# Layer 0's first weights loaded behind x's second tile, their high parts written by Pool and their low parts by VectorE, and the first zT half in two column parts

## The chip, the cores and the metric

The kernel runs as one program on one core of a Trainium2 chip. The metric is the device time of one launch in microseconds (us), the median of three runs; lower is better.

## What is computed

A trunk of two layers on 1024 tokens of width 1024, all in float32. Cut to what matters here:

```python
for l in range(DEPTH):                       # DEPTH = 2
    h = _rmsnorm(x, g_pre_mix[l])
    z = h @ w_in[l]                          # 1024 x 1280
    zf, zq, zk, zv, zm = jnp.split(z, splits, axis=-1)   # zf: the first 256 columns
    y_f = _fourier_mix(zf, w_fourier[l])     # FFT over tokens and channels, then w_fourier
    ...                                      # windowed attention on zq, zk, zv
    mkv = _rmsnorm(mem, g_mem[l]) @ w_mem_kv[l]          # keys and values of 256 memory rows
    ...                                      # memory attention with zm, then w_out and a residual
    ...                                      # SwiGLU with w_ffn_in, w_ffn_out and a residual
```

The change concerns the first of these products alone: `zf`, the first 256 columns of `h @ w_in[0]`, in layer 0.

## The kernel before

**Products in three passes.** TensorE multiplies in a rounded 32-bit format (`fp32r`). To keep precision, each operand is kept as a high part, its rounding, and a low part, what the rounding left. A product is three matmuls: high by high, high by low, low by high (`Acc.add`, L173). `split` (L160 to 163) makes the two parts: ScalarE (ACT) casts the high part (L162), and VectorE (DVE) or GpSimd (POOL) subtracts it for the low part (L163).

**The start of layer 0.** x comes in eight tiles of 128 tokens (`start_load`, L1339; five slots). For each, `start_tile` (L1343) squares and sums the tile on ACT (L311), turns the sum into a scale on POOL (L313, L314), and transposes the tile on TensorE in two groups of four 128x128 blocks, `hTp` (L325). Each group is split by ACT (L162) and DVE (L163) into the two parts of hT. Four tiles make a half of hT, 512 tokens wide.

The gain g_pre_mix is folded into the weights. `zf_load` (L521) calls `load_w` (L355): four transfers of 256 KB, each two k-blocks of 128 rows by 256 columns, into a ring of three raw slots (`raws`, L136). POOL scales each block in place (`scaled`, L353), ACT casts the high part of the pair, POOL subtracts for the low part, and only then is the slot free for a later load. The transfers stand behind x's fourth tile, and a fourth one behind the small tables and x's later tiles.

`zf(0)` (L524) then makes zT, 256 rows by 512 tokens: two row blocks of 24 matmuls each, 512 columns wide, then a split, then `pq` (a small product with the Fourier tables that `fourier_tables`, L503, has made through `abp`). The second half, `zf(1, 2)`, is made in two column parts of 256 tokens.

Between the two halves stands the memory's work (`Memory.make`, L472): two tiles of mem are loaded, squared (L300), normed on DVE (L305) and transposed (`mTp`, L450); eight transfers of w_mem_kv go through the same ring of three raw slots, each cast on ACT and subtracted on DVE; `kmp` and `vmp` are the products. Then `kvz_load` takes eight more blocks of w_in through the same ring (`load_w512`, L375: ACT and DVE for the even blocks, POOL and ACT for the odd ones).

**What sets the order.** The program is written as a sequence, and a scheduler then orders the instructions of each engine by a timeline of its own. Each engine runs its list in that order: an instruction that waits holds up what stands behind it. All loads named here are issued by SyncE (SP). From its ninth transfer on, SP waits before each issue for the transfer issued eight places before, and where a buffer is reused also for the engine that last read it. PSUM buffers come in pairs per tag (L42): `sc` holds zT, `pT` holds abp, mTp and pq, `pd` holds hTp, kmp and vmp.

Of the kernel before, what the change touches and what calls it, by code (L numbers as in the profile page):

```python
# [12 lines left out]
F32R = mybir.dt.float32r  # L13
# [3 lines left out]
ALU = mybir.AluOpType  # L17
AX = mybir.AxisListType

P = 128  # L20
# [38 lines left out]
def weave(*streams):  # L59

    order = []
    for si, units in enumerate(streams):
        order += [((i + 0.5) / len(units), si, i, u) for i, u in enumerate(units)]
    for *_, u in sorted(order, key=lambda o: o[:3]):
        u()
# [3 lines left out]
def tile_encoder(ctx: ExitStack, tc: tile.TileContext, T, C, out):  # L69
    nc = tc.nc  # L70
# [32 lines left out]
    def shaped(ap, shape):  # L103
        names = "abcde"[: len(shape)]
        dims = {c: d for c, d in zip(names, shape)}
        return ap.rearrange(f"p ({' '.join(names)}) -> p {' '.join(names)}", **dims) if len(shape) > 1 else ap

    def at(k, *shape, dt=F32):

        t = arenas[F32R if dt is F32R else F32]  # L110
        if dt is not F32R and k >= 8:
            k, t = (k - 8, flex["t"]) if k < 16 else (k - 8, t)
        o = int(k * 256)
        ap = t[:, o : o + math.prod(shape)]
        return shaped(ap.bitcast(dt) if dt is I32 else ap, shape)
# [16 lines left out]
    def run(k, n, step):  # L132
        return Ring(*[k + i * step for i in range(n)])


    raws, junks = run(0, 3, 2), Ring(56)  # L136
# [20 lines left out]
    f32 = lambda ap: ap.bitcast(F32)  # L157
    mm = nc.tensor.matmul

    def split(hi, lo, src, lo_eng=None):  # L160

        nc.scalar.copy(hi, src)  # L162
        return (lo_eng or nc.vector).tensor_tensor(out=lo, in0=src, in1=f32(hi), op=ALU.subtract)  # L163
# [16 lines left out]
    def cst(*shape):  # L180
# [20 lines left out]
        out=mask[:, 0:P], in_=mask[:, 0:P], pattern=[[1, P]], compare_op=ALU.is_ge,  # L201
# [4 lines left out]
        out=mask[:, 2 * P : 3 * P], in_=mask[:, 2 * P : 3 * P], pattern=[[-1, P]],  # L206
# [101 lines left out]
    def token_scale(x, t):  # L308

        ss = sm(1, "nss")  # L310
        nc.scalar.activation(junks(D // 2).bitcast(BF16), x, AF.Square, accum_out=ss)  # L311
        v = sm(1, "nrsv")
        nc.gpsimd.tensor_scalar(out=v, in0=ss, scalar1=1.0 / D, scalar2=EPS, op0=ALU.mult, op1=ALU.add)  # L313
        nc.gpsimd.tensor_tensor(out=rx[:, t : t + 1], in0=v, in1=mhalf[:, 0:1], op=ALU.pow)  # L314

    def norm_T(h, hT, t, tag="pd"):

        half, c = divmod(t, 4)
        if c == 0:
            hT[half] = [[at(32 * half + 16 * i + 8 * kg, 4, 512, dt=F32R) for kg in range(2)] for i in range(2)]  # L320
        for kg in range(2):
            pt = ps([4, P], "hTp", tag)
            for j in range(4):
                k = kg * 4 + j
                nc.tensor.transpose(pt[:, j, :], h[:, k * P : (k + 1) * P], ident)  # L325
            split(hT[half][0][kg][:, :, c * P : (c + 1) * P], hT[half][1][kg][:, :, c * P : (c + 1) * P], pt)
# [25 lines left out]
    def scaled(raw, g, k):  # L352
        nc.gpsimd.tensor_scalar(out=raw, in0=raw, scalar1=g[:, k : k + 1], scalar2=1.0, op0=ALU.mult, op1=ALU.mult)  # L353

    def load_w(w, c0, n, k, lo_eng=None, g=None):  # L355


        kn = 1024 // n
        kr = kn // 2
        res = []  # L360
        for k0 in range(0, NK, kn):
            hi, lo = at(k, kn, n, dt=F32R), at(k + 4, kn, n, dt=F32R)
            k += 8
            for j in range(0, kn, kr):
                raw = raws(kr, n)
                r0 = (k0 + j) * P
                nc.sync.dma_start(raw, w[r0 : r0 + kr * P, c0 : c0 + n].rearrange("(k p) c -> p k c", p=P))
                if g is not None:
                    for i in range(kr):
                        scaled(raw[:, i], g, k0 + j + i)  # L370
                split(hi[:, j : j + kr], lo[:, j : j + kr], raw, lo_eng)
            res += [(hi[:, i], lo[:, i]) for i in range(kn)]
        return res
# [122 lines left out]
    class Mix:  # L496
# [22 lines left out]
            self.PQ = {}  # L519

        def zf_load(self):  # L521
            self.wzf = load_w(self.win, 0, 256, 64, nc.gpsimd, self.g)

        def zf(self, half, parts=1):  # L524

# [813 lines left out]
    def start_load(t):  # L1339
        hx[t] = at(32 + 4 * (t % 5), D)  # L1340
        nc.sync.dma_start(hx[t], x_in[t])

    def start_tile(t):  # L1343

        token_scale(hx[t], t)
        norm_T(hx.pop(t), hT, t)
        if t + 5 < NT:
            start_load(t + 5)
# [3 lines left out]
    mix = Mix(0, hT, mem)  # L1352
    start_load(0)
    gains_T(gpT, T["g_pre_mix"], at(15, P))
    for t in range(1, 4):
        start_load(t)
    mix.zf_load()
    start_load(4)
    for t in range(4):
        start_tile(t)  # L1360
    mix.fourier_tables(58)
    prep()
    mem.make()
    weave([lambda t=t: start_tile(t) for t in range(4, 8)], [lambda: mix.zf(0)])

    for l in range(DEPTH):
        mix.zf(1, 2)
# [57 lines left out]
        if l + 1 < DEPTH:  # L1425
            mem = Memory(l + 1, 16, 0, 16, 28, "pT")
            mix = Mix(l + 1, nhT, mem)
# [83 lines left out]
```

## Time and profile before

| | |
|---|---|
| median of 3 runs | 2069.59 us (2065.72 to 2076.48) |
| the profiled execution | 2072.77 us |
| its span, first to last instruction | 2070.9 us |
| mean granted TensorE clock | 0.981 |
| TensorE (PE) busy | 2001.5 us, 97% |
| VectorE (DVE) busy | 1546.8 us, 75% |
| ScalarE (ACT) busy | 1061.7 us, 51% |
| GpSimd (POOL) busy | 714.1 us, 34% |

The 1.9 us between the profiled execution's own time and its span lie around the instructions. PE is matmul; PEld is the loading of a weight block into TensorE, which overlaps PE. In a row of the timeline stand the start, the length (of all the instructions that the row merges), the engine, the line, the operation, output and input, the shape, and the count; in square brackets stands the idle time before it and what ended it. PEclk is the clock that TensorE was granted, as a share of full speed. SPq rows are issues of transfers, not the transfers.

### The profile page before, as it was taken

How to read it: one execution, taken by the hardware profiler on the slowest of the kernel's cores; microseconds unless marked ns; L12 is line 12 of the kernel's file. 1: busy time of each engine (PE TensorE's matmuls, PEld its weight loads, DVE VectorE, ACT ScalarE, POOL GpSimd, SP SyncE). 2: the span in 40 equal slices, each digit the busy share in tenths (PEclk: the TensorE clock that was granted, in tenths of full speed). 3: DMA queues.
4: the chain of work that ended last, by engine and by line, in shares of the span. 5: the costliest groups of instructions: out<-in, count | busy, mean ns of one | idle time of the engine just before them, and what ended most of it. 6: DMA issues, size and time to landing. Idle time of an engine off the chain costs nothing.

```text
span 2070.9 us, 28456 instructions
## 1 busy us (share of the span) xinstructions
PE 2001.5 (97%) x9587; PEld 1638.0 (79%) x9587; DVE 1546.8 (75%) x2496; ACT 1061.7 (51%) x2250; POOL 714.1 (34%) x819
## 2 busy tenths in 40 slices
PE   7999999899999999999999989997999999999998
PEld 6877777678888888887888768775888888878886
DVE  5556767888787786768876776579887787778767
ACT  6466777643333333455545677775433333345542
POOL 4354445433343333002423544363342342320002
PEclk9999999899999999999999999998999999999999
DMA  6110222423233233879841122233332233269974
GB/s 212 48 57 31 103 97 102 143 77 107 89 120 97 97 112 104 297 266 332 281 175 39 57 67 93 83 123 121 97 126 95 87 132 97 97 217 342 305 257 155
DMA packets 173634, 286.47 MB, mean 138 GB/s; under 512 B 15496, under 2 KB 73392, under 8 KB 173488
## 3 DMA queue, kind: packets, MB, share of 16 engines
q1 hardware_dynamic: 165424, 265.78, 38.7%
q10 hardware_dynamic: 8064, 18.88, 2.4%
q8 instruction: 75, 1.23, 0.2%
q14 instruction: 71, 0.58, 0.1%
HBM read 218.02 MB, written 66.58 MB: 137 GB/s over the span
## 4 chain that ended last, share of the span: by engine, by line
PE 85%; DVE 4%; DMA 3%; ACT 3%; POOL 3%; issue 2%; SPq 0%; DVEq 0%; POOLq 0%; ACTq 0%
PE fo L1277 19%; PE qz L1142 12%; PE qx L1142 11%; PE qy L1142 11%; PE mo L173 7%; PE qw L1142 6%; PE kvp L173 4%; PE qp L173 4%; PE zT L173 2%; PE pT L808 2%; PE sc L771 1%; DVE arena_r L163 1%; PE av L823 1%; PE av L816 1%; PE mav L916 1%
## 5 line engine op out<-in xcount | busy, mean ns | idle before, releaser
L162 ACT CAST arena_r<-arena_f 128x512 fp32r<-128x512 f32 (+2 forms) x714 | 411.5, 598 | 631.1 <-PE qz L1142 119.8
L163 DVE TENSOR_TENSOR arena_r<-arena_f,arena_r 128x512 fp32r<-128x512 f32 x632 | 476.5, 775 | 138.0 <-ACT arena_r L162 129.7
L1277 PE MATMUL fo<-arena_r 128*128 128x512 f32 x1848 | 424.7, 391 | 5.8 <-ACT arena_r L162 5.8
L1277 PEld LDWEIGHTS fo<-arena_r 128*128 128x128 f32 x1848 | 347.0, 188 | 78.8 <-ACT arena_r L162 4.4
L1142 PE MATMUL qy<-arena_r 128*128 128x512 f32 x1056 | 263.7, 400 | 16.5 <-ACT arena_r L162 11.1
L1142 PEld LDWEIGHTS qy<-arena_r 128*128 128x128 f32 x1056 | 203.3, 193 | 62.6 <-ACT arena_r L162 11.8
L1132 DVE TENSOR_TENSOR arena_f<-arena_f 128x512 f32<-128x512 f32 x220 | 201.9, 924 | 11.5 <-DMA arena_f<-in_w_ffn_in 5.0
L1142 PE MATMUL qz<-arena_r 128*128 128x512 f32 x704 | 199.1, 395 | 2.5 <-ACT arena_r L162 1.9
L1162 POOL TENSOR_TENSOR arena_f<-arena_f 128x512 f32<-128x512 f32 x44 | 71.8, 1633 | 313.7 <-ACT arena_f L1147 313.7
L1142 PEld LDWEIGHTS qz<-arena_r 128*128 128x128 f32 x704 | 134.2, 191 | 31.9 <-ACT arena_r L162 2.6
L1142 PE MATMUL qx<-arena_r 128*128 128x512 f32 x528 | 127.9, 390 | 0.4 <-ACT arena_r L162 0.4
L1142 PE MATMUL qw<-arena_r 128*128 128x512 f32 x528 | 127.3, 389 | 0.0
L1142 PE MATMUL qx<-big,arena_r 128*128 128x512 f32 x528 | 126.8, 389 | 0.0
L1142 PEld LDWEIGHTS qx<-arena_r 128*128 128x128 f32 x528 | 99.2, 188 | 21.7 <-ACT arena_r L162 1.2
L1142 PEld LDWEIGHTS qx<-big,arena_r 128*128 128x128 f32 x528 | 99.1, 188 | 20.6
L1142 PEld LDWEIGHTS qw<-arena_r 128*128 128x128 f32 x528 | 99.1, 188 | 20.6
L1142 PE MATMUL qz<-big,arena_r 128*128 128x512 f32 x352 | 115.2, 389 | 0.0
L221 POOL TENSOR_SCALAR rrsv<-rss 128x1 f32<-128x1 f32 x32 | 17.7, 554 | 259.3 <-ACT arena_f L334 207.3
L173 PE MATMUL qp<-big,arena_r 128*128 128x512 f32 x384 | 99.5, 404 | 2.0 <-POOL big L163 2.0
L173 PE MATMUL mo<-big,arena_r 128*128 128x512 f32 x384 | 101.4, 400 | 0.0
L1194 POOL TENSOR_TENSOR arena_f<-arena_f,flex 128x512 f32<-128x512 f32 x32 | 52.5, 1640 | 139.7 <-DVE arena_f L1174 101.0
L173 PE MATMUL mo<-arena_r 128*128 128x512 f32 x384 | 100.2, 401 | 0.3 <-POOL arena_r L163 0.3
(245 smaller groups left out, 3532.8 us busy)
## 6 DMA issues: line engine op xcount, KB each, us to landing
arena_f<-in_w_ffn_out SPq DMA_DIRECT2D x264, 256.0 KB, 4.6
arena_f<-in_w_ffn_in SPq DMA_DIRECT2D x88, 512.0 KB, 3.6
actd<-arena_f SPq DMA_DIRECT2D x154, 256.0 KB, 3.7
arena_f<-actd SPq DMA_DIRECT2D x154, 256.0 KB, 4.6
arena_f<-in_w_in SPq DMA_DIRECT2D x40, 256.0 KB, 2.8
arena_f<-in_x SPq DMA_DIRECT2D x16, 512.0 KB, 4.8
arena_f<-in_w_out SPq DMA_DIRECT2D x32, 256.0 KB, 2.7
pmd<-arena_f ACTq DMA_DIRECT2D x32, 256.0 KB, 2.0
```

The source lines that it names most:

```text
L162: nc.scalar.copy(hi, src)
L163: return (lo_eng or nc.vector).tensor_tensor(out=lo, in0=src, in1=f32(hi), op=ALU.subtract)
L173: mm(self.dst, a, b, start=self.i == 0, stop=self.i == self.n - 1)
L771: mm(pt, lhs, self.kst[g][i][:, k0 * P : k1 * P], start=i == 0, stop=i == 1)
L808: nc.tensor.transpose(pT[:, h, :], es_[h // 2][:, h % 2, j * P : j * P + P], ident)
L816: mm(av[64 * s : 64 * s + 64, 0 : 2 * P], self.v32[:, k0 + j], rhs, start=j == 0, stop=j == nk - 1)
L823: mm(av, lhs, p_, start=j == 0 and i == 0, stop=j == nk - 1 and i == 1)
L1132: nc.vector.tensor_tensor(out=s, in0=a, in1=b, op=op)
L1142: mm(pt, a, b, start=start and n == 0, stop=n == 11, skip_group_check=not start)
L1162: nc.gpsimd.tensor_tensor(out=self.v, in0=self.v, in1=self.s2, op=ALU.add)
L1194: (G if i in (0, 3) else V).tensor_tensor(out=a[i], in0=c, in1=g[i], op=ALU.mult)
L1277: mm(pt, ab[:, 0, x, sl], ab[:, 1, y], start=new and first and j == 0, stop=last and j == 2, skip_group_check=not new)
```

## The change

The weights of layer 0's `zf` no longer go through `load_w`. For each block of 128x256, POOL's scaling writes its product straight into the high part's `fp32r` buffer, and DVE makes the low part in one instruction, raw times gain minus high part. ACT has no part in it, and the scaling in place and POOL's subtraction are gone. Layer 1 keeps `load_w`. The loads are called behind x's second tile rather than behind its fourth, and `zf(0)` becomes `zf(0, 2)`: two parts of 256 tokens, so 96 matmuls of 256 columns in the place of 48 of 512.

```diff
         def zf_load(self):
-            self.wzf = load_w(self.win, 0, 256, 64, nc.gpsimd, self.g)
+            if self.l:
+                self.wzf = load_w(self.win, 0, 256, 64, nc.gpsimd, self.g)
+                return
+            self.wzf = []
+            for k0 in (0, 4):
+                hi, lo = at(64 + 2 * k0, 4, 256, dt=F32R), at(68 + 2 * k0, 4, 256, dt=F32R)
+                for j in (0, 2):
+                    raw = raws(2, 256)
+                    r0 = (k0 + j) * P
+                    nc.sync.dma_start(raw, self.win[r0 : r0 + 2 * P, 0:256].rearrange("(k p) c -> p k c", p=P))
+                    for i in range(2):
+                        g = self.g[:, k0 + j + i : k0 + j + i + 1]
+                        h = hi[:, j + i]
+                        nc.gpsimd.tensor_scalar(out=h, in0=raw[:, i], scalar1=g, scalar2=1.0, op0=ALU.mult, op1=ALU.mult)
+                        nc.vector.scalar_tensor_tensor(
+                            out=lo[:, j + i], in0=raw[:, i], scalar=g, in1=f32(h), op0=ALU.mult, op1=ALU.subtract
+                        )
+                self.wzf += [(hi[:, i], lo[:, i]) for i in range(4)]
...
     start_load(0)
     gains_T(gpT, T["g_pre_mix"], at(15, P))
-    for t in range(1, 4):
+    start_load(1)
+    mix.zf_load()
+    for t in range(2, 5):
         start_load(t)
-    mix.zf_load()
-    start_load(4)
     for t in range(4):
         start_tile(t)
...
-    weave([lambda t=t: start_tile(t) for t in range(4, 8)], [lambda: mix.zf(0)])
+    weave([lambda t=t: start_tile(t) for t in range(4, 8)], [lambda: mix.zf(0, 2)])
```

The scheduler answers with another order on every engine, over about the first fifth of the program and in a small stretch of layer 1. Lines of the changed kernel behind L538 are 17 higher than before.

On TensorE, at the start of the program, before (hTp_5 and 6 are x's first tile, 9 and 10 its second, 13 and 14 its third, 17 and 18 its fourth; zT_48 and zT_49 are the two row blocks of zT; abp the Fourier tables):

```order
L325 MATMUL hTp_10_168<-const_81,arena_f_73 128x128 x4
L325 MATMUL hTp_13_181<-const_81,arena_f_73 128x128 x4
L514 MATMUL abp_19_218<-arena_f_73 128x64
L514 MATMUL abp_20_224<-arena_f_73 128x64
L325 MATMUL hTp_14_188<-const_81,arena_f_73 128x128 x4
L325 MATMUL hTp_17_201<-const_81,arena_f_73 128x128 x4
L514 MATMUL abp_21_231<-arena_f_73 128x64
L514 MATMUL abp_22_237<-arena_f_73 128x64
L173 MATMUL zT_48_494<-arena_r_72 128x512
L173 MATMUL zT_49_521<-arena_r_72 128x512
L325 MATMUL hTp_18_208<-const_81,arena_f_73 128x128 x4
```

And of the changed kernel, from the same row on:

```order
L325 MATMUL hTp_10_168<-const_81,arena_f_73 128x128 x4
L173 MATMUL zT_48_494<-arena_r_72 128x256
L173 MATMUL zT_49_521<-arena_r_72 128x256
L325 MATMUL hTp_13_181<-const_81,arena_f_73 128x128 x4
L173 MATMUL zT_48_494<-arena_r_72 128x256 x11
L173 MATMUL zT_49_521<-arena_r_72 128x256 x8
L173 MATMUL zT_48_494<-arena_r_72 128x256
L173 MATMUL zT_49_521<-arena_r_72 128x256 x2
L325 MATMUL hTp_14_188<-const_81,arena_f_73 128x128 x4
L173 MATMUL zT_48_494<-arena_r_72 128x256 x5
L514 MATMUL abp_19_218<-arena_f_73 128x64
L514 MATMUL abp_20_224<-arena_f_73 128x64
```

zT's first matmuls moved from behind the fourth tile's first transposes and all four abp to right behind the second tile's; 28 of the 96 narrow ones stand before the first abp.

On ACT, further on, before (mTp are the transposes of the memory; the casts of arena_f 128x512 are those of w_mem_kv, whose eight transfers are here called kv0 to kv7, but for the second of the first row's three, which is the fourth pair of w_in's blocks; so that row is kv0, w_in, kv1):

```order
L162 CAST arena_r_72<-arena_f_73 128x512 x3
L162 CAST arena_r_72<-mTp_29_316 128x4x128
L162 CAST arena_r_72<-mTp_30_323 128x4x128
L162 CAST arena_r_72<-arena_f_73 128x512
L162 CAST arena_r_72<-mTp_34_337 128x4x128
L162 CAST arena_r_72<-arena_f_73 128x512 x2
L162 CAST arena_r_72<-zT_48_494 128x512
L162 CAST arena_r_72<-zT_49_521 128x512
L162 CAST arena_r_72<-mTp_35_344 128x4x128
```

And of the changed kernel, where kv0 and kv1 have been cast further up (the first row is kv2 to kv4; zT_52 and zT_53 are the second column part):

```order
L162 CAST arena_r_72<-arena_f_73 128x512 x3
L162 CAST arena_r_72<-zT_52_564 128x256
L162 CAST arena_r_72<-arena_f_73 128x512
L162 CAST arena_r_72<-zT_53_591 128x256
L162 CAST arena_r_72<-arena_f_73 128x512
L162 CAST arena_r_72<-mTp_29_316 128x4x128
L162 CAST arena_r_72<-mTp_30_323 128x4x128
L162 CAST arena_r_72<-arena_f_73 128x512
L162 CAST arena_r_72<-mTp_34_337 128x4x128
L390 ACTIVATE big_72_812<-arena_f_73,const_81 128x512
L162 CAST arena_r_72<-mTp_35_344 128x4x128
```

Before, the casts of the first two mTp stand behind those of kv0 and kv1; now they stand behind those of kv0 to kv6, and zT's casts stand ahead of them.

## Prediction

> **What bounds the kernel now.** I read the page first, then the waits of TensorE, then windows of 20 us.
>
> ```profile
> span 2070.9 us, 28456 instructions
> PE 2001.5 (97%) x9587; PEld 1638.0 (79%) x9587; DVE 1546.8 (75%) x2496; ACT 1061.7 (51%) x2250; POOL 714.1 (34%) x819
> ```
>
> PE is busy all but 69.4 us of the span, so a change in the order of loads can win no more than a part of that, and what half clock costs. Where these lie near the change, the windows tell (PE busy, PEld, DVE, ACT, POOL, granted clock, share of the DMA engines, GB/s):
>
> ```profile
> 0.00:20.00 20.00, 10.30 (x45) 8.51 (x45) 7.22 (x20) 14.41 (x31) 12.62 (x29) 0.84 0.88 287
> 20.00:40.00 20.00, 18.84 (x98) 15.90 (x99) 15.69 (x29) 13.76 (x27) 7.85 (x13) 0.91 0.54 172
> 40.00:60.00 20.00, 16.68 (x122) 16.44 (x121) 10.77 (x18) 12.86 (x24) 9.10 (x12) 0.86 0.48 145
> 140.00:160.00 20.00, 17.08 (x85) 14.53 (x86) 16.57 (x32) 11.96 (x35) 7.93 (x12) 0.91 0.01 2
> ```
>
> In the first 20 us PE stands idle for 9.7, in the next 1.2, in the third 3.3. DMA is close to full in the first window (0.88) and about half used in the next two. 0.5% of the time is 10.3 us, about what a measurement of this kernel can tell from no change: the whole idle time of the first 20 us is less than that.
>
> **The start.** These rows of the timeline carry the first two terms.
>
> ```profile
> 7.23 1.06 ACT L311 ACTIVATE arena_f<-arena_f 128x1024 bf16<-128x1024 f32 x1 [0.74 <-DMA arena_f<-in_x]
> 9.84 0.33 SPq L240 DMA_DIRECT2D const<-in_sink  x1
> 10.60 0.33 SPq L438 DMA_DIRECT2D arena_f<-in_mem  x1
> 10.88 1.85 POOL L353 TENSOR_SCALAR arena_f<-arena_f,const 128x256 f32<-128x256 f32 x4
> 11.93 0.69 DVE L163 TENSOR_TENSOR arena_r<-hTp,arena_r 128x512 fp32r<-128x512 f32 x1 [0.83 <-ACT arena_r L162]
> 15.74 2.50 POOL L163 TENSOR_TENSOR arena_r<-arena_f,arena_r 128x512 fp32r<-128x512 f32 x2
> 17.71 1.22 PE L173 MATMUL zT<-arena_r 128*128 128x512 f32 x2 [1.17 <-ACT arena_r L162]
> 19.92 7.03 PE L173 MATMUL zT<-arena_r 128*128 128x512 f32 x22
> 20.41 1.28 DVE L305 SCALAR_TENSOR_TENSOR arena_f<-arena_f,nrs 128x1024 f32<-128x1024 f32 x1 [1.12 <-issue]
> 25.84 0.94 POOL L353 TENSOR_SCALAR arena_f<-arena_f,const 128x256 f32<-128x256 f32 x2
> 29.94 0.42 DVE L274 SCALAR_TENSOR_TENSOR flex<-flex 128x256 f32<-128x256 f32 x1
> 31.13 3.02 PE L173 MATMUL zT<-arena_r 128*128 128x512 f32 x12
> 34.34 0.36 PE L173 MATMUL kmp<-arena_r 128*128 128x256 f32 x1
> ```
>
> x's second tile is there at 7.2. The issues at 9.84 and 10.60 wait for the transfers eight places ahead, x's fourth tile and the first w_in pair, so these landed by 9.8 and 10.6: a pair of 256 KB takes about 0.7 us of a full DMA. Behind the second tile, the first pair lands near 7.8, the second near 8.5, the third near 10.6; the fourth waits for a slot and lands, by my count of the bytes in the queue, near 14.6.
>
> What goes: on POOL two of its steps become one, so the subtraction goes (1.25 us each, 4 of them); on ACT four casts go, 0.62 each. What comes: on DVE eight low parts of 128x256 at 0.42, 3.4 us, in a window in which it is 36% busy. A block's high part costs POOL 0.46 as before. PE gets 96 narrow matmuls for 48 wide ones: 3.02/12 is 0.252 for a wide one, a narrow one takes 0.133 (2.52/19, row below), 0.7 us more in all.
>
> Followed through the new order by these durations (all estimates): the second tile's second transposes wait until DVE has made the low part ahead of them, which now stands behind two weight low parts, and end at 10.5; zT starts there and not at 17.7. It doesn't run through: the third tile's transposes wait for a PSUM buffer until 11.5 and 15.0; the third abp waits for ACT, which stands behind mem's second tile (landing near 16.1, sum of squares 1.06 more), until 19.6. The first column part ends at 21.4. The second needs zT's PSUM buffer, whose low part stands on DVE behind the two L305 of 1.28, and so starts at 23.6 and ends at 29.8. Before, zT ended at 34.15 (31.13 and 3.02). PE is 4.3 us ahead there, less 0.9 to 1.2 for mTp transposes that before lie inside: **3.2 us ahead**, not 7.
>
> **The mTp wait.** The lead meets the ring of raw slots.
>
> ```profile
> 34.22 0.37 SPq L367 DMA_DIRECT2D arena_f<-in_w_mem_kv  x1
> 36.95 0.62 ACT L162 CAST arena_r<-arena_f 128x512 fp32r<-128x512 f32 x1 [0.16 <-DMA arena_f<-in_w_mem_kv]
> 31.00 3.69 DMA arena_f<-in_w_mem_kv
> 37.76 1.84 PE L173 MATMUL kmp<-arena_r 128*128 128x256 f32 x14
> 43.76 5.92 PE L173 MATMUL vmp<-arena_r 128*128 128x256 f32 x48
> ```
>
> A w_mem_kv transfer takes 2.7 us (34.22 to 36.95) to 3.7 from issue to use, even with an idle DMA. In the new order ACT casts kv2 to kv6 ahead of the first mTp. kv2's cast stands behind four sums of squares of x's tiles and ends near 28.4; kv5 takes kv2's slot, is issued near 29.1 and lands, at 2.9, near 32.0; kv6 near 33.1; then come two mTp casts, and the third mTp, which needs the first's PSUM buffer, runs at 35.9. PE has had nothing since 30.9: a new wait of about 5 us. kmp starts at 37.1 against 34.34. What follows on PE to vmp is 66 narrow matmuls at 0.131 (1.84/14), 8.7 us, and some 1.5 us of waits for mTp's low parts: vmp starts near 47 and not 43.76, before the clock is counted.
>
> **The clock.** How PE comes out of such a gap, this trace shows at 52 us:
>
> ```profile
> 50.67 1.04 PE L325 MATMUL hTp<-const,arena_f 128*128 128x128 f32 x8
> 51.52 0.62 ACT L162 CAST big<-arena_f 128x512 fp32r<-128x512 f32 x1 [2.57 <-POOL arena_f L353]
> 55.03 0.79 PE L173 MATMUL zT<-arena_r 128*128 128x256 f32 x2 [3.32 <-ACT arena_r L162]
> 55.62 1.91 PE L325 MATMUL hTp<-const,arena_f 128*128 128x128 f32 x8
> 57.18 4.91 PE L173 MATMUL zT<-arena_r 128*128 128x256 f32 x24
> 62.28 2.52 PE L173 MATMUL zT<-arena_r 128*128 128x256 f32 x19
> 54.00:56.00 2.00, 0.97 (x4) 0.98 (x5) 1.29 (x2) 1.81 (x5) 1.44 (x2) 0.61 0.80 241
> 56.00:58.00 2.00, 2.00 (x12) 2.00 (x11) 0.41 (x1) 2.00 (x5) 0.98 (x1) 0.50 0.22 64
> 60.00:62.00 2.00, 2.00 (x14) 2.00 (x14) 0.05 (x1) 0.00 (x0) 0.00 (x0) 0.69 0.26 77
> 62.00:64.00 2.00, 2.00 (x19) 2.00 (x18) 0.69 (x1) 0.71 (x2) 0.00 (x0) 1.00 0.00 0
> ```
>
> After 3.32 us without work the granted clock is 0.50 and comes back near 61.3, some 6 us after work resumed. It costs 1.7 us on the 24 matmuls (4.91 less 24 at 0.133), 0.9 on the transposes (1.91 less 1.04) and 0.5 on the first two: 3.1. The Trainium skill, TensorE: Matmul & The Clock Gate, Part 1, has the clock halved after an idle window of about 3.4 us and given back after about 3.4 us of sustained work; by that page the price is 1.7 us and not 3.1. The trace disagrees on the way back, and I take the trace, a little shortened, since part of the new half-clock time is waiting anyway: 2.5 us. vmp then starts at 47 to 48.5, say 47.5: **3.7 us behind**.
>
> **What is given back.** The gap of 3.32 us at 52 comes from ACT, which stood at a cast of the next w_in blocks (51.52, waiting 2.57 for POOL). By the ring's count these blocks come 4 to 6 us earlier now (their first load is issued when kv5's slot is free, near 33.4), while vmp ends later, near 53.4; so ACT has them behind it. In the new order four hTp stand in a row behind vmp, and two pq copies stand between their casts on ACT: about 1.5 us of waiting stays. So 3.3 and 3.1 go and 1.5 come: 4.9 us won. From 3.7 behind that is 1.2 ahead, and the 0.7 for narrow matmuls is in the durations used.
>
> From 62 us on PE is dense up to 140 us, so the lead is carried there. There it meets this:
>
> ```profile
> PE ms L884 <- ACT flex L409: 2.3, 1, 2.3
> PE ms L884 <- DVE flex L411: 0.9, 1, 0.9
> ```
>
> The new order puts two `ms` and then 21 `qp` where eight `ms` stood: the second of these waits has work in front of it and goes, 0.9 us; the first stays. Sum: 1.2 and 0.9, **2.1 us won, say 2.5** with the ends below on both sides. On the profiled execution's own 2072.8 that is 2070.3; the median of the runs stands 3.2 lower, so 2067.1.
>
> Other edits cost nothing: the later x tiles and g_mem (their squares are on ACT behind work that ends later), the small tables on SP, POOL's scale factors; their cover is the abp wait until 19.6, and without it each would cost its own 0.2 to 0.6. The reordering of the first 400 us has no row of its own; PE's idle time from 140 to 160, 2.9 us, is the nearest, and I give it that on each side.
>
> **The rivals.**
>
> *The lead is kept.* If kv5 and kv6 land before ACT asks for them, the mTp wait is gone. For it: DMA is nearly idle then (0.54 over 20 to 40 us), and the scheduler set the casts so. Against it: every such transfer here took 2.7 to 3.7. kmp then starts near 32.5, vmp near 41.5, 2.3 ahead; 4.9 and 0.9 more are 8.1 won, 2061.5; if the abp wait at 18.1 to 19.6 and the one for zT's buffer also go, 11 won, 2058.6. It takes a transfer of about 1.9 us or less, or ACT running later than I have it. The Trainium skill, DMA: Bandwidth & Descriptors, Anatomy of one DMA, gives about 2.0 us and the bytes at 436 GB/s per transfer, for POOL's issue path; for 256 KB that would be an estimated 2.6 us, which shortens the wait by 0.3 to 1.1 but does not remove it. The trace's shortest, 2.7, agrees with it; its longest doesn't.
>
> *Slower.* The mTp wait takes the lead and nothing is given back: vmp starts 3.7 behind, and behind it ACT again stands at a cast of w_in when the hTp need it, so PE has its 3.3 us gap and the 3.1 us of half clock after it as before. It decides where the eight w_in blocks come later than vmp's end near 53.4, that is where a turn of the ring takes over 6 us and not the 4.4 (2.9 for the transfer, a cast, a low part) that I count. 3.7, the 1.5 of waiting between the hTp casts, and 2.9 for the reordering are 8.1 lost: 2077.7.
>
> *Nothing moves.* The zT start doesn't come earlier because POOL and DVE hold each other up, or the wait at 52 stays as it is and merely the gaps change place: 2069 to 2071.
>
> **How the numbers follow.** Forecast 0.52, lead kept 0.23, nothing moves 0.13, slower 0.12. The forecast's own range takes the transfer at 2.7 or 3.7 (1 us either way, twice through the ring) and 2.9 for the reordering: 2062 to 2073. The range to hold 8 in 10 reaches to the kept lead's low end and the slower case: 2058.5 to 2077.5. Faster by over 0.5% means below 2059.3: half of the kept lead at its best, 0.11. Slower means above 2079.9: half of the slower case, 0.06. Within it 0.83.
>
> **What would show it.** Right: zT begins near 10.5; the first zT part's end near 21, the second's near 30; a gap on PE of 3 to 6 us before the third mTp, put down to ACT, followed by a granted clock of 0.5; kmp at 36 to 38; no gap over 2 us at 52 to 60. Wrong: kmp before 34 (kept lead), a gap of 3 us behind vmp with clock 0.5 (slower), zT beginning behind 15. If all these stand as forecast and the time is off by over 5 us, the reordering behind 140 us has decided, which the idle time of PE there would show.

## The result, and the profile after

The changed kernel is 0.6% slower. Its median is 2086.1 us (10 runs, 2076.91 to 2089.25) beside 2071.4 us for the kernel before on the same chip (10 runs, 2065.72 to 2076.58): a ratio of 1.0058, with a 95% interval of 1.0042 to 1.0074. The forecast of 2067.1 and its range up to 2077.5 both missed it. The profiled execution took 2085.91 us with a span of 2084.1, 13.2 more than the span of before.

The page of the changed kernel:

```profile
span 2084.1 us, 28560 instructions
PE 2005.1 (96%) x9635; PEld 1645.6 (79%) x9635; DVE 1547.3 (74%) x2506; ACT 1059.9 (51%) x2248; POOL 711.5 (34%) x815
```

PE is busy for 3.6 us more than before and idle for 79.0 instead of 69.4, which is 9.6 more. The four windows that the prediction showed, now of the changed kernel (same columns):

```profile
0.00:20.00 20.00, 13.32 (x81) 12.44 (x82) 8.77 (x22) 12.22 (x24) 11.11 (x30) 0.91 0.85 284
20.00:40.00 20.00, 13.59 (x96) 12.80 (x95) 18.60 (x40) 15.32 (x35) 6.43 (x11) 0.91 0.68 220
40.00:60.00 20.00, 16.21 (x128) 15.97 (x127) 9.42 (x13) 11.77 (x22) 9.13 (x11) 0.91 0.34 108
140.00:160.00 20.00, 17.92 (x85) 14.67 (x84) 17.76 (x32) 12.15 (x32) 7.92 (x12) 0.91 0.04 13
```

In the first 20 us PE has 3.0 us more work done than before, as wanted. In the next 20 it stands idle for 6.4 us instead of 1.2, so the lead is gone at 40 us. The rows of PE's timeline say where (start, busy time, then the group; in brackets the idle time before it and what ended it):

```profile
8.79 0.47 PE L173 MATMUL zT<-arena_r 128*128 128x256 f32 x2 [0.25 <-ACT arena_r L162]
18.75 1.68 PE L173 MATMUL zT<-arena_r 128*128 128x256 f32 x12
22.05 1.85 PE L173 MATMUL zT<-arena_r 128*128 128x256 f32 x13 [0.67 <-DVE arena_r L163]
25.95 4.46 PE L173 MATMUL zT<-arena_r 128*128 128x256 f32 x35 [1.90 <-DVE arena_r L163]
30.25 1.47 PE L450 MATMUL mTp<-const,arena_f 128*128 128x128 f32 x12
35.57 0.53 PE L173 MATMUL kmp<-arena_r 128*128 128x256 f32 x2 [3.85 <-DVE arena_r L163]
45.55 5.92 PE L173 MATMUL vmp<-arena_r 128*128 128x256 f32 x48
52.04 1.91 PE L325 MATMUL hTp<-const,arena_f 128*128 128x128 f32 x16
57.74 0.79 PE L173 MATMUL zT<-arena_r 128*128 128x256 f32 x2 [3.79 <-ACT arena_r L162]
```

zT starts 8.9 us earlier than before, the keys' first matmul (kmp) 1.2 us later, the values (vmp) 1.8 later, and the second half of zT 2.7 later (55.03 before). Both long waits are followed by half the clock:

```profile
36.00:38.00 2.00, 2.00 (x11) 2.00 (x10) 2.00 (x5) 1.24 (x2) 0.30 (x1) 0.50 0.44 131
58.00:60.00 2.00, 2.00 (x10) 2.00 (x11) 1.01 (x2) 0.75 (x2) 0.00 (x0) 0.50 0.00 0
62.00:64.00 2.00, 2.00 (x14) 2.00 (x14) 0.00 (x0) 0.01 (x1) 0.00 (x0) 0.69 0.00 0
```

Followed by the last instruction of each kind on PE, the changed kernel lags by 1.9 us in these two profiles at 66 us (the last of x's transposes) and still by 1.9 at 198 (the last qp, the product for the queries). At 218 us (the last mav, the memory attention's product with its values) the lag is 8.1, and 8.7 from 394 to 834. Layer 1 adds some: 10.5 at 894, 11.7 at 1022, 11.4 at 1847. The step of 6.2 us between 198 and 218 has these rows (mpT are transposes of the memory attention's weights), first of the changed kernel:

```profile
209.78 1.07 PE L933 MATMUL mav<-arena_f 128*64 128x512 f32 x2 [1.04 <-ACT arena_f L925]
211.80 0.50 PE L788 MATMUL sc<-arena_r 128*128 128x256 f32 x2 [0.51 <-ACT arena_f L907]
214.06 0.80 PE L788 MATMUL sc<-arena_r 128*128 128x256 f32 x2 [1.76 <-ACT arena_f L907]
210.00:220.00 10.00, 7.73 (x31) 6.35 (x30) 8.61 (x26) 7.52 (x19) 3.76 (x6) 0.67 0.47 149
```

and of the kernel before:

```profile
209.45 1.07 PE L916 MATMUL mav<-arena_f 128*64 128x512 f32 x2 [1.43 <-ACT arena_f L908]
210.00:220.00 10.00, 9.03 (x45) 5.26 (x43) 8.42 (x26) 8.11 (x22) 2.40 (x5) 1.00 0.43 136
```

In the changed order the scores (sc) of the next stage stand on PE ahead of the last transposes of the memory's weights, and they wait for ACT. No single wait is over 1.8 us, yet the granted clock falls to 0.67 over 10 us and PE gets 31 matmuls done there, not 45.

### The profile page after: what moved, and what is told of

Same layout as the page of the kernel before. It is cut to its first block, busy times and chain, and to the rows that moved or that the text cites. A ratio compares the mean times of both kernels' runs of the same rounds, so it can differ in the third digit from the quotient of the medians.

```text
span 2084.1 us, 28560 instructions
## 1 busy us (share of the span) xinstructions
PE 2005.1 (96%) x9635; PEld 1645.6 (79%) x9635; DVE 1547.3 (74%) x2506; ACT 1059.9 (51%) x2248; POOL 711.5 (34%) x815
## 4 chain that ended last, share of the span: by engine, by line
PE 80%; DMA 6%; DVE 5%; ACT 3%; POOL 2%; issue 2%; SPq 0%; DVEq 0%; POOLq 0%; ACTq 0%
PE fo L1294 13%; PE qz L1159 11%; PE qx L1159 11%; PE qy L1159 11%; PE mo L173 7%; PE qw L1159 6%; PE kvp L173 4%; PE qp L173 4%; DMA arena_f<-actd 3%; DVE arena_r L163 2%; PE sc L788 2%; PE zT L173 2%; PE pT L825 2%; ACT arena_r L162 1%; DMA arena_f<-in_w_ffn_out 1%
## 5 line engine op out<-in xcount | busy, mean ns | idle before, releaser
L1149 DVE TENSOR_TENSOR arena_f<-arena_f 128x512 f32<-128x512 f32 x220 | 201.0, 919 | 11.4 <-DMA arena_f<-in_w_ffn_in 4.9
```

The source lines that it names most:

```text
L1149: nc.vector.tensor_tensor(out=s, in0=a, in1=b, op=op)
```

## The experiments

**How an order is held.** The scheduler answers any edit with another order on every engine. To tell the edit from the order, a kernel's order is pinned: edges without a semaphore from each instruction to the next one on its engine, from a table of instruction numbers. The helper is the same in all kernels below that pin an order; only the table differs.

```diff
+def _pin(tc, table, shift):
...
+            i = by[f"I-{n + shift}"]
+            if prev is not None:
+                tc.add_manual_dep(
+                    i, prev.name, mybir.DependencyInfo(mybir.DependencyClass.NoSync, mybir.DependencyReason.DATA), reason="order"
+                )
...
+        _pin(tc, _ORDER, 54)
```

"The start" is everything up to the keys, the values and the first half of zT. "The later order" is all from the second half of zT and its loads on; its instructions are the same in both kernels, so it can be given to either start.

All comparisons in one table. "Clock" is the part of the mean difference that goes with the granted clock: time x (1 - mean granted clock), averaged over a kernel's runs, less the same for the kernel before, run beside it on the same chip. It counts low clock while PE is idle too, so it is an upper bound.

| kernel | start | later order | median, before's | ratio, 95% interval | mean difference, of it clock |
|---|---|---|---|---|---|
| late_as_before | changed | before | 2083.10, 2074.59 | 1.0048, 1.0029 to 1.0066 | +9.4, +3.9 |
| late_as_after | before | changed | 2079.94, 2074.59 | 1.0024, 1.0010 to 1.0039 | +5.1, +5.8 |
| waits_moved | changed, waits moved | before | 2084.79, 2074.59 | 1.0048, 1.0030 to 1.0066 | +9.8, +3.9 |
| load_early | early load alone | before | 2077.19, 2075.47 | 1.0009, 0.9992 to 1.0026 | +2.3, -0.4 |
| split_only | split alone | before | 2077.86, 2075.47 | 1.0007, 0.9993 to 1.0021 | +2.0, 0.0 |
| two_parts | two parts alone | before | 2073.70, 2075.47 | 0.9992, 0.9976 to 1.0009 | -1.6, -3.0 |
| to_230_as_after | before | changed up to 230 us | 2078.84, 2075.47 | 1.0012, 0.9995 to 1.0029 | +3.3, +1.0 |
| zt_behind | changed, zT behind transposes | before | 2082.83, 2075.64 | 1.0045, 1.0032 to 1.0057 | +8.0, +4.0 |
| early_split | two edits | before | 2077.79, 2075.64 | 1.0015, 1.0001 to 1.0028 | +2.9, +3.8 |
| early_parts | two edits | before | 2077.14, 2075.64 | 1.0012, 0.9999 to 1.0024 | +2.1, +0.7 |
| split_parts | two edits | before | 2077.56, 2075.64 | 1.0016, 1.0004 to 1.0028 | +2.1, +3.8 |
| mtp_first | changed, mTp ahead | before | 2080.46, 2073.34 | 1.0040, 1.0024 to 1.0056 | +6.9, +3.8 |
| mtp_zt | both of these | before | 2081.66, 2073.34 | 1.0055, 1.0033 to 1.0078 | +9.5, +5.7 |
| x_first | changed, SP's loads set | before | 2076.21, 2073.34 | 1.0018, 1.0000 to 1.0037 | +3.3, +2.2 |
| from_230_as_after | before | changed from 230 us | 2082.75, 2073.34 | 1.0058, 1.0038 to 1.0078 | +9.7, +6.4 |
| x_first_again | as x_first | before | 2078.30, 2074.30 | 1.0019, 0.9999 to 1.0038 | +3.4, +2.1 |
| late_as_before_again | changed | before | 2085.87, 2074.30 | 1.0051, 1.0032 to 1.0071 | +10.6, +6.7 |

### Start or later order

The first theory was the last sentence of the prediction, that the reordering behind 140 us had decided; the rival was that the start costs.

late_as_before, the changed kernel with the later order of before:

> The changed kernel with its own start (up to the second half of zT and the loads of the next w_in blocks), and everything behind that in the order that the kernel before has on each engine. Order theory (of the 13.2 us that the profile lost, only the 1.8 us by which vmp is late come from the start, the rest from the new order of stages that the edit does not touch, where PE's waits lie closer together and pull the granted clock down): 2 to 4 us slower than before. Start theory (a start that is late by 2 us grows through the later stages in whatever order): 10 to 13 us slower, like the changed kernel.

late_as_after, the kernel before with the later order of the changed one:

> The kernel before with its own start, and everything behind it in the order of the changed kernel. Order theory: 8 to 11 us slower than before, though not one instruction differs. Start theory: within 2 us of before.

waits_moved, late_as_before with the order of the start changed on PE, ACT and DVE so that PE's two waits should go (some of the mTp transposes and their casts earlier, the hTp casts ahead of the pq copies):

> As late_as_before, and within the start three things in another order: the memory's first transposes on PE ahead of the second column part's second row block, their casts on ACT ahead of those of w_mem_kv's third to seventh transfers, and the hTp casts behind vmp ahead of the two pq copies that wait for the store of the memory's keys and values. Order theory with the two waits found in the trace (3.85 us before kmp, 3.79 us behind vmp): both go, with some of their half clock, so 5 to 9 us faster than late_as_before and 2 to 6 us faster than before. Rival (the casts and transfers behind them are late in any order): within 2 us of late_as_before.

before_again, the kernel before with its own order, once:

> The kernel before once more, for a second profile. If its stages agree with the first profile within 0.5 us each, the differences between two profiles can be read stage by stage; if the stages at the turn from the first to the second product of the feed-forward part differ by 1 to 3 us, the 1.8 us that the changed kernel lost there is no effect of the change.

The changed start costs 9.4 us (10.6 when repeated), the later order 5.1. Neither theory alone has it: about two thirds of the loss is made in the start, a third behind it. In the start's loss 3.9 of 9.4 (6.7 of 10.6) goes with the clock, the rest is other waiting; that of the later order may be clock alone (at most 5.8, of 5.1). Moving the two waits changed nothing that can be measured, but it hardly removed them either. In the profile of waits_moved PE waits 1.37 us before kmp (4.64 in late_as_before), but 3.82 ahead of zT's second part (0.73 and 2.31), and behind vmp 1.45, 2.73 and 0.98 (3.86): 10.4 us in all, 11.5 in late_as_before.

before_again took 2070.6 us, and its profile shows what the prediction's base was worth. The row that has a wait of 3.32 us in the profile of before, and a window behind it, read:

```profile
52.15 0.51 PE L173 MATMUL zT<-arena_r 128*128 128x256 f32 x2 [2.32 <-ACT arena_r L162]
54.00:56.00 2.00, 2.00 (x20) 2.00 (x19) 1.33 (x2) 1.60 (x3) 1.30 (x1) 1.00 0.04 12
```

The wait is 2.32 us and the clock stays at 1.00. Five profiled executions have this start; their waits at this place are 3.32, 2.32, 1.74, 1.58 and 4.54 us (before, before_again, late_as_after, to_230_as_after, from_230_as_after), and the clock of the 14 us from 50 to 64 is 0.76, 1.00, 1.00, 1.00 and 0.76. At 66 us they stand at 0, -5.8, -5.1, -4.4 and -0.5 us beside the profile of before. With the changed start the wait is 3.79, 3.86 and 4.52 (the changed kernel, late_as_before and its repeat), each time with half clock, and they stand at +1.9, +6.1 and +2.1. So the means, -3.2 and +3.4, are some 6.5 us apart, where the first two profiles differ by 1.9.

### One edit at a time

```diff
-    for t in range(1, 4):
-        start_load(t)
-    mix.zf_load()
-    start_load(4)
+    start_load(1)
+    mix.zf_load()
+    for t in range(2, 5):
+        start_load(t)
```

That is load_early; split_only has only the new body of `zf_load`, two_parts only `mix.zf(0, 2)`. The start is ordered by the scheduler anew each time, the later order is pinned as in before.

> Only the first of the three edits: the four loads of w_in's first weights stand behind x's second tile; the weights are split as before (Pool scales, ScalarE casts, Pool subtracts) and the first half of zT stays one part. Everything from the second half of zT on has the order of before. Theory L (loads): 1 MB ahead of x's tiles 3 to 5 delays them, and since each load of SP waits for the eighth before it to land, a 512 KB tile of x in the place of a 256 KB weight block delays the memory's tiles and x's last tiles too; then this kernel alone has most of the loss of the changed start: 2079 to 2084 us beside 2074 for before, 4 to 8 us late at the hTp of 66 us. Rival S (split) and rival P (two parts): the load alone costs nothing, 2072 to 2077.

> Only the second edit: Pool's scaling writes the high parts, VectorE the low parts, with the loads behind x's fourth tile as before and zT's first half in one part; later order as before. Theory L: no loss, 2071 to 2077 (ScalarE loses four casts of 0.6 us, VectorE gains eight of 0.55). Rival S: VectorE's eight subtracts stand ahead of what frees the key weights' buffers and of the memory's low parts, 2078 to 2083.

> Only the third edit: zT's first half in two column parts, loads and split as before; later order as before. Theory L: no loss, 2072 to 2077. Rival P: TensorE meets a second wait between the parts and ScalarE's casts are put in another order, 2078 to 2083.

None of them costs as much as 4 us by its mean, and theory L, which gave the loss to the early load alone, fell. split_only's median, 2077.86, lies between the ranges of its two theories. Two parts alone are the one edit whose mean is below before, by 1.6 us with an interval that holds zero.

### Two edits at a time, and TensorE's order

zt_behind is late_as_before with PE's order of the start pinned otherwise; the scheduler orders the other engines around that row. early_split, early_parts and split_parts leave one edit out each.

> All three edits, later order as in before; only TensorE's order in the start is another: the first column part of zT (24 + 24 matmuls) stands behind all transposes of x's tiles 3 to 5 and the abp blocks, not ahead of them; SP's loads keep the order of the changed start. None of the three edits alone cost over 4 us, all three about 10. Theory E (TensorE's order): with both early weights and two parts, zT's matmuls run ahead of the transposes that free x's buffers and feed ScalarE, so the chain to the keys and values is late; then this kernel loses at most 4 us: 2073 to 2079 beside 2075 for before. Rival Q (SP's order): the last tiles of x stand behind the first key weights and the fourth block of w_in; that order is unchanged here, so 2081 to 2086.

> Two of the three edits: loads behind x's second tile and the split on Pool and VectorE; zT's first half in one part, so its matmuls wait for x's fourth tile and stand behind the transposes on TensorE. On SP two blocks of key weights stand ahead of x's last tiles, as in the changed start. Later order as in before. Theory E: 2073 to 2079. Rival Q: 2080 to 2086.

> Two of the three edits: loads behind x's second tile and zT's first half in two parts; the weights are split as before. TensorE has 16 of zT's matmuls ahead of the transposes of x's fourth and fifth tiles; on SP the memory's tiles stand ahead of the fourth block of w_in, two key blocks ahead of x's last three tiles. Later order as in before. Theory E: the loss of the changed start comes back, 2079 to 2085. Rival Q: about half of it at most, 2075 to 2080.

> Two of the three edits: the split on Pool and VectorE and two parts; the loads stay behind x's fourth tile in the program. TensorE has 22 of zT's matmuls ahead of the transposes of x's fourth tile, as in the changed start; on SP x's tiles 5 to 7 stand ahead of the key weights. Later order as in before. Theory E: 2079 to 2085. Rival Q: 2073 to 2077.

Theory E fell: with zT behind the transposes the loss stays, 1.0045. Rival Q named zt_behind and early_parts rightly, had split_parts half a microsecond too low, and named early_split wrongly (1.0015 where it wanted 1.003 and more). early_parts tests it less than its expectation says: in its profile SP issues one block of key weights, not two, ahead of x's last tile alone. By their means, any two edits cost 2 to 3 us, all three 9.4 (10.6 when repeated). What zt_behind waits for is not zT:

```profile
39.91 0.80 PE L173 MATMUL kmp<-arena_r 128*128 128x256 f32 x2 [5.11 <-ACT arena_r L162]
```

### The loads' order on SP, and the memory's transposes

In the changed start the chain of waits runs through the loads, here in late_as_before (start, duration, what):

```profile
4.06 9.09 DMA arena_f<-in_x
...
13.17 6.38 DMA arena_f<-in_mem
...
19.62 7.99 DMA arena_f<-in_x
...
27.70 1.16 ACT arena_f L311 x2
```

and SP's own queue in that run:

```profile
13.17 0.33 SPq L438 DMA_DIRECT2D arena_f<-in_mem  x1
...
14.53 0.38 SPq L367 DMA_DIRECT2D arena_f<-in_w_mem_kv  x1
14.96 0.51 SPq L1358 DMA_DIRECT2D arena_f<-in_x  x1
...
16.71 1.07 SPq L367 DMA_DIRECT2D arena_f<-in_w_mem_kv  x1
19.62 0.80 SPq L1358 DMA_DIRECT2D arena_f<-in_x  x2
```

The second tile of the memory is issued when x's fourth tile, eight loads ahead of it, has landed (4.06 and 9.09 are 13.15), and x's last two tiles when that memory tile, eight loads ahead again, has landed (19.55). In the kernel before, SP issued x's last tile at 14.83. There the place eight ahead of a memory tile was held by 256 KB of w_in; now it is held by 512 KB of x, and two blocks of key weights and the fourth pair of w_in stand ahead of x's last tiles. x's last square then starts on ACT at 29.20 and not at 24.47, and ACT, which works in order, has key casts and the memory's casts behind it. In the profile of before, SP's issue and the square were:

```profile
14.83 0.45 SPq L1341 DMA_DIRECT2D arena_f<-in_x  x1
24.47 1.06 ACT L311 ACTIVATE arena_f<-arena_f 128x1024 bf16<-128x1024 f32 x1
```

This profile has the latest loads of the three with the changed start: the last square starts at 26.94 in the changed kernel and at 26.70 in late_as_before_again.

mtp_first, mtp_zt and x_first set the start's order on one engine each in late_as_before: the memory's transposes on PE, these and zT's first part, or SP's loads. The scheduler orders the other engines around that row. In mtp_first it moves SP's second block of key weights ahead of one more tile of x; in x_first it also puts half of the mTp transposes ahead of zT's second part and the hTp casts ahead of the pq copies.

> All three edits, later order as in before. TensorE's order in the start: the memory's 16 transposes (mTp) stand behind the first 13 matmuls of zT's second column part, not behind all 48; TensorE waited 2.3 us there anyway. Theory M: the loss of the changed start is mTp standing behind zT's second part, so the keys' first matmul is late; then kmp starts 3 to 5 us earlier than with the changed start (38.5 us) and the time is 2074 to 2079 beside 2075 for before. Rival Q (the loads' order on SP, unchanged here) and any rival on the loads: 2081 to 2086.

> As the kernel before in this list, and zT's first part also stands behind the transposes of x's tiles and abp. Theory M: 2074 to 2079. Rival: 2081 to 2086.

> All three edits, later order as in before; only SP's order of the loads in the start is set: the memory's tiles and x's tiles 5 to 8 stand ahead of the fourth block of w_in and of all key weights; the other engines are ordered around that. Rival Q: the loss of the changed start is x's last tiles waiting behind the key weights; then the last squares of x on ScalarE come 2 to 4 us earlier than at 29.2 us and the time is 2073 to 2078. Theory M alone: half of the memory's transposes also come ahead of zT's second part here, so 2076 to 2081. Neither: 2081 to 2086.

> The source of before with the order of before up to about 230 us, behind that the order of the changed kernel. The later order as a whole gave 1.0024, the part up to 230 us 1.0012. If the loss behind the start lies at the scores of 205 to 226 us alone: 0.999 to 1.001, 2073 to 2077. If it is spread: 1.001 to 1.003, 2077 to 2082.

The two rows that x_first's expectation asks for, SP's last tile of x and its square on ACT:

```profile
16.70 0.33 SPq L1358 DMA_DIRECT2D arena_f<-in_x  x1
25.84 1.06 ACT L311 ACTIVATE arena_f<-arena_f 128x1024 bf16<-128x1024 f32 x1
```

The square comes 3.4 us earlier than in late_as_before, but only 0.9 and 1.1 earlier than in the other two profiles of the changed start. The ratio is 1.0018 where the changed order had 1.0048. Theory M alone asked for 2076 to 2081, so x_first's 2076.21 lies in its range as in rival Q's. mtp_first speaks against theory M: it stays at 1.0040, its median of 2080.46 between the two ranges, though PE's rows show the keys far earlier. vmp starts 5.7 us earlier than in the changed kernel (39.86), the second half of zT only 1.7:

```profile
56.07 0.79 PE L173 MATMUL zT<-arena_r 128*128 128x256 f32 x2 [7.60 <-ACT arena_r L162]
```

mtp_zt stays at 1.0055, in the rival's range. So theory M fell as the cause of the whole; a part of 3 us or so can't be told from none. To set the two orders of SP side by side, both kernels ran once more on one chip:

> The kernel x_first once more, beside late_as_before once more on the same chip. Rival Q (the order of the loads on SP makes the changed start slow): 1.000 to 1.0025 of before, and 5 us or more under late_as_before. If SP's order has no part in it, both give 1.003 to 1.006.

> The kernel late_as_before once more: all three edits with the start as in the changed kernel and the later order of before. Both theories: 1.003 to 1.0065 of before; the question is what stands beside it.

1.0019 and 1.0051, medians 7.6 us apart. The order of the loads on SP, with what the other engines make of it, carries 6 to 7 of the start's 10 us (9.4 less 3.3, 10.6 less 3.4); which of these consequences counts most was not told apart.

The profiles put that gain into the start as well. Beside the profile of before, vmp ends 4.3 to 5.7 us early in the two profiles of x_first and 1.6 to 5.6 late in the three with the changed start; at 66 us it is 2.6 to 2.9 early against 1.9 to 6.1 late. PE still waits behind vmp in x_first, 4.34 and 3.29 us, with half clock after it:

```profile
50.97 0.80 PE L173 MATMUL pq<-arena_r 128*128 128x256 f32 x2 [4.34 <-ACT arena_r L162]
```

That x's last tiles are what costs is not shown, and two profiles speak against it: the last square starts at 31.48 in early_parts and at 29.52 in split_parts, later than in the changed start, and each loses 2 us only. What differs more in x_first is the memory's chain: its transposes start at 22.74 us (30.25 in the changed kernel) and kmp at 31.26 (35.57).

No version is faster than before: the best, two_parts, can't be told from it.

### Where the later order costs

to_230_as_after and from_230_as_after split the later order at about 230 us.

> The source of before, its start in the order of before; from there to about 230 us the order of the changed kernel, behind that the order of before again. The later order as a whole cost about 5 us (2079.9 beside 2074.6). Theory: it is one place, the scores behind the memory's last sums at 205 to 226 us, where TensorE stands 2 to 3 us in pieces and its clock falls: then this kernel has it all, 2078 to 2082, and the last mav ends 6 to 7 us later against its start. Rival: the loss is spread over the later stages, then 2073 to 2076.

The profile of to_230_as_after has the stage at 205 to 226 us as the changed kernel has it, with waits of 1.13, 0.51, 1.14 and 0.36 and the clock down:

```profile
206.00:216.00 10.00, 8.38 (x39) 6.27 (x38) 8.36 (x27) 8.62 (x23) 3.87 (x6) 0.83 0.45 136
```

From the last qp to the last mav it falls back by 5.4 us beside before, late_as_after by 5.6, the changed kernel by 6.2; in the profiles of the kernels with before's order of this stage it moves by less than 1. The place is real. But part of these steps is only work that changed places, since scores that stood behind the last mav now stand ahead of it. At the layer's last score, at 366 us, to_230_as_after has lost 2.3 us since the last qp and late_as_after 2.6; the changed kernel has lost 6.8, with more half clock behind 300 us. So the place isn't the whole of the later order's 5 us: timed, to_230_as_after loses 1.0012, with an interval that holds zero, and from_230_as_after, which doesn't have that place, 1.0058, more than the whole later order. The pieces don't add up. Most of from_230_as_after's loss goes with the clock (6.4 of 9.7), and its profile has it in layer 1 (lag 2.1 at 894 us, 6.7 at 1240, 7.0 at 1847). One profile can't lay that on the order: of these, 3.4 us come between 1232 and 1240, and load_early and split_only, which have before's order there, fall back by 3.3 and 3.4 at the same place. from_230_as_after also lies outside both of its ranges. What does it is left open.

## Why the prediction was wrong, point by point

The prediction had the start 1.2 us ahead and 0.9 won behind it. Timed apart, the start lost 9.4 (10.6 when repeated) and what lies behind it 5.1. The steps that failed are the gap behind vmp that it counted as won, the x tiles that it counted as costing nothing, and the size of the reordering.

**zT's start and its two parts: right within 2 us.** Forecast 10.5 for the start, 21.4 for the end of the first part, 23.6 to 29.8 for the second; measured 8.79, 20.4, 22.05 to 30.4. The second part was stopped once more than forecast, 1.90 us, for the low part of a transposed tile that stood behind the two L305 on DVE.

**The mTp wait: right that it comes, wrong on what waits, and smaller.** Forecast a wait of 5 us before the third mTp, for the first one's PSUM buffer, and kmp at 37.1; measured 3.85 before kmp, at 35.57. Three of the four mTp groups ran in a row from 30.25, before ACT read the first at 33.44, so the third didn't need that buffer back. The forecast 35.9 for the third is when the fourth ran (35.91), which is luck. The two key-weight casts that waited for their transfers did so until 30.2 and 32.1, where 32.0 and 33.1 had been counted, and what ended PE's wait was a low part on DVE behind ACT's casts. The step also called the DMA idle around these transfers; by its own window it was half used from 20 to 40 us (0.54), and in the changed kernel it was 0.68 there.

**The clock behind it: right.** 0.50 at 36 to 38, back at 40; vmp 1.8 behind instead of 3.7.

**"What is given back": this step failed.** It let the gap of 3.32 us at 52 and its half clock go, and counted 4.9 us won. The gap is still there, 3.79 us, with half the clock behind it, which the prediction had named as a sign of being wrong. The reason that the step gave for the gap did go: the last cast of a w_in block starts at 50.41, ahead of vmp's end, as forecast. What it then saw as "two pq copies" with 1.5 us of waiting is this, in ACT's timeline of the changed kernel:

```profile
52.24 0.69 ACT L569 ACTIVATE arena_f<-pq,const 128x512 f32<-128x512 f32 x1 [0.35 <-PE pq L173]
52.82 1.06 ACT L162 CAST arena_r<-hTp 128x512 fp32r<-128x512 f32 x2
55.95 1.26 ACT L569 ACTIVATE arena_f<-pq,const 128x512 f32<-128x512 f32 x2 [2.06 <-DMA kvd<-arena_f]
57.10 1.07 ACT L162 CAST arena_r<-hTp 128x512 fp32r<-128x512 f32 x2
```

The pq copies write where the store of the keys and values (kvd) still reads; the store goes out behind vmp and lands 2.97 us later, at 55.86, and the two hTp casts that zT needs stand behind the copies. In the kernel before the copies wait for that store as well, but with those casts ahead of them:

```profile
53.89 1.08 ACT L162 CAST arena_r<-hTp 128x512 fp32r<-128x512 f32 x2
55.17 1.27 ACT L552 ACTIVATE arena_f<-pq,const 128x512 f32<-128x512 f32 x2 [0.19 <-DMA kvd<-arena_f]
```

A wait of 2.57 us was taken off ACT, and the next one in the same queue, 2.06, took its place. The rival "slower" had the place and the gap, by the wrong cause (it asked for late w_in casts), and its 2077.7 was still too small.

**The base: the second failure.** The 3.32 us and the 3.1 of half clock were read from one execution. Of five profiled executions with that start, three have a shorter wait there and no half clock at all. So in those three most of the 4.9 us "given back" was not there to be won, and a loss was hidden: against the one profile the changed start is 1.9 us late at 66 us, against the mean of five 5.1.

**The loads ahead of it: missed.** The prediction put the later x tiles at nothing, because ACT squares them behind work that ends later. It had itself read from two rows that SP's issues wait for the loads eight places ahead, and didn't follow that on: the fourth tile of x moved into such a place, and through the memory's second tile it holds x's last two tiles to 17 to 20 us. That the loads' order on SP carries 6 to 7 us of the loss, with what the other engines make of it, was shown by x_first and its repeat. By which path it costs stays open: the chain above was a reading of one profile, and early_parts and split_parts don't bear it out.

**The second `ms` wait: right and worth nothing.** It is gone from the list of PE's waits, and the lag is 1.8 us at 137 and 1.9 at 198. In before_again it was 0.6 us, not 0.9.

**The reordering, 2.9 us on each side: too small.** It was named as without a row. Timed alone it is 5.1 us, which may be clock alone. One stage, the scores behind 205 us, has 2.3 and 2.6 of it in the two profiles that have before's start, and 6.8 in the changed kernel; the rest has no place that the runs show. The prediction's last sentence gave the reordering a miss of over 5 us if all its signs stood. They didn't, since the gap behind vmp was there, and the reordering has a third of the loss, the start the rest.

## What to carry to other kernels

Earlier work on the busiest engine wins only if the chain that feeds its next step is not pushed back for it: follow each moved load through the rule that decides when the following loads may be issued, not only through its own bytes. Before a gap is booked as won, look for the next wait behind it in the same queue, and read the gap in more than one execution, since the same wait can be there with half clock behind it in one run and shorter, at full clock, in the next. With a scheduler behind the code, pin the order of what an edit doesn't touch, or its price is mixed with that of every instruction moved with it.

## What the runs showed of the hardware

- One and the same program spreads by 20 us, and the granted clock goes with it in part: of 28 runs of before on one chip, the three at a mean clock of 0.988 took 2063 to 2071 us, the two at 0.979 took 2077 and 2083.
- At the wait behind vmp the clock fell to half where the wait was 3.32 us or longer (five executions of the two starts, up to 4.54) and stayed at 1.00 where it was 2.32 or shorter (three). The Trainium skill, TensorE: Matmul & The Clock Gate, Part 1, halves the clock after at least one idle window of about 3.4 us. As a rule on the length of a wait this does not hold here: load_early waits 3.44 us at that place and keeps 1.00, early_split waits 2.87 and has 0.50 from 58 to 60 us, and the wait of 2.25 us at 140 us of before is followed by 0.50 from 144 to 146.
- At 209 to 214 us of the changed kernel the clock fell without a wait over 1.76 us: PE was busy 0.96, 1.49 and 0.30 us in the three windows of 2 us from 208 to 214, and the clock was 1.00, 1.00 and 0.85 there, 0.50 in the next. An idle window of 3.4 us would not have given that. The same page, in its section on a second HAM failure mode, has a kernel in which short idle times between groups of matmuls make the clock swing; the rows here agree with that, at 2.75 us of work in 6.
- In the changed kernel work resumed at 57.74, and the clock was 0.50 up to 62 and 0.69 from 62 to 64, so it came back some 5.5 us later. Counted from the shares in the windows of 2 us (0.60 from 56 to 58), half clock lasted from 56.4 to 63.2, 6.8 us, and in before from 54.4 to 61.3 as well. The same Part 1 gives the clock back after a busy window of about 3.4 us and calls these windows free-running; work that starts inside one would then have to fill the next, and two windows are 6.8. The rows agree with that. So the prediction's 1.7 us read the page too short, and the 3.1 that it took from the rows is near half of 6.8.
